# A decoder trunk's first feed-forward: the norm's weights into the transposed input, each token's scale into the results

## The chip, the cores and the metric

The kernel runs on one core of a Trainium2 chip. The metric is the device time of one execution in microseconds, as a median over runs. In the text TensorE does the matrix products, VectorE and ScalarE the elementwise work, GpSimd little beside powers and constants, and SyncE issues the transfers.

## The reference

Two layers run over 256 tokens of width 1024, all in float32. Each layer has a feed-forward, a mixer (a gated recurrence beside windowed attention), a second feed-forward and a gated embedding. Only the start is touched by the change, apart from one move that all four feed-forwards share:

```python
def rmsnorm(x, g):
    xf = x.astype(jnp.float32)
    y = xf * lax.rsqrt(jnp.mean(xf * xf, axis=-1, keepdims=True) + EPS)
    return (y * g.astype(jnp.float32)).astype(x.dtype)

def swiglu(x, w_gate, w_up, w_down):
    return (jax.nn.silu(x @ w_gate) * (x @ w_up)) @ w_down

h = h + 0.5 * swiglu(rmsnorm(h, ffn1_norm), ffn1_w_gate, ffn1_w_up, ffn1_w_down)
```

The scale of a token, the inverse root of its mean square, is one number per row of the input. So it can be applied before the products or to their results; the weight vector `g` has one number per feature, which is a row of the transposed input.

## The kernel before

A product of float32 numbers is made of three faster ones. Every operand is split into a high part (`wh` of the weights, `uT` and so on of the activations; a cast on ScalarE) and a low part (`wl`; a subtraction on VectorE), and TensorE adds high x high, high x low and low x high (`mm3`, line 392; `mm3s`, line 444). So every megabyte of weights is loaded by SyncE into one of two `raw` buffers, split into `wh` and `wl` in pieces of 1024 columns (`feed`, line 332; a ring of 8 pieces), and used by TensorE. A `raw` buffer is loaded anew when VectorE has made the low part of its last piece.

The order of the work on each engine is fixed when the program is written out. A clock of estimated costs (`Clock`, line 61) goes along; background chains (`later`, line 214; `tick`, line 199) are advanced when that clock has passed their ready time, and between two matmuls `feed` splits the next piece of weights if the clock allows.

The program starts in `opening` (line 528). SyncE issues the first 128 rows of x in two halves, the norm's weight vector broadcast over 128 partitions (`gain`, line 523: `g`, 512 KB), the first megabyte of gate weights in four pieces of 256 KB, the other 128 rows of x, and the second megabyte in two pieces. TensorE runs twelve products on a constant tile (`heat`). The mean square of the first rows comes from ScalarE (`sumsq`, line 587) and VectorE, the power from GpSimd (`scale`, line 596), then VectorE makes the normalised rows `xn` (`scaled`, line 603), TensorE transposes them in blocks of 128, and they are split into `uT`. The same is done for the other 128 rows while the first are already multiplied.

The feed-forward (`ffn`, line 653) has three kinds of units. The first 512 features are done with tokens on the partitions: `by_token` (line 663) multiplies a gate unit and an up unit (both named `gu`), applies silu and the product on the results `sg`, and has them transposed by TensorE later (`later_T`, line 519). For the first six pieces `project` (line 398) does the first 128 tokens of a whole unit and then the second. The features behind it come in units of 512 with features on the partitions (`by_feature`, line 694): a gate unit `pg`, silu on ScalarE straight from PSUM (`silu`, line 688), an up unit `pu`, and the product on VectorE (`swiglu`, line 676), which is split into `hid`. There are four full pairs of such units, one of 128 features and a last one of 64. Then the down product `dn` runs over 22 pieces of rows of `w_down` (`down_run`, line 726), at whose start the small loads for the following block are issued.

## Time and profile before

| what | us |
|---|---|
| median of 3 runs (1367.38 to 1368.12) | 1367.64 |
| the profiled execution | 1368.5 |
| its span, first to last instruction | 1366.7 |
| TensorE busy (matmuls) | 1356.1 |
| VectorE busy | 877.4 |
| ScalarE busy | 727.6 |
| first product of the feed-forward starts at | 10.88 |

The page of the profile names engines PE (TensorE's matmuls), PEld (its weight loads), DVE (VectorE), ACT (ScalarE), POOL (GpSimd) and SP (SyncE; SPq is its queue of transfers). L131 is the line of the wrapper that records nearly every instruction, so that rows are told apart by their tiles: `wh<-raw` is the high part of weights made from a loaded buffer. A row of the timeline gives the start, the duration, the engine, the operation, the tiles, the shape and a count, and in brackets the idle time of the engine before it with what ended that. A row of the waits gives who waited for whom, the sum, how often, and the longest. A row of the windows gives for each engine the busy time and the number of instructions, then the clock granted to TensorE as a share of full speed, the busy share of the DMA engines, and what they moved in GB/s.

### The profile page before, as it was taken

To read this page: it belongs to the slowest core of one execution; us is meant where nothing else is said; L and a number is where in the kernel's file an instruction comes from. 1 tells how busy PE (TensorE), PEld (TensorE's weight loads), DVE (VectorE), ACT (ScalarE), POOL (GpSimd) and SP (SyncE) were. 2 spreads that over 40 slices of the span, in tenths; PEclk is the share of its full clock that TensorE was granted. 3 is DMA by queue.
4 is the path that set the end of the run, shared out by engine and by line. 5 is a ranking of instruction groups with operands and counts; after the bars stand their busy time and mean duration, and the time that the engine had idled before them with its cause. 6 is when DMAs were issued, how large, how long until landed. Compare 5 with 4: busy or idle time off the path is not lost.

```text
span 1366.7 us, 21958 instructions
## 1 busy us (share of the span) xinstructions
PE 1356.1 (99%) x9018; PEld 1228.8 (90%) x9018; DVE 877.4 (64%) x1323; ACT 727.6 (53%) x1155; POOL 57.0 (4%) x86
## 2 busy tenths in 40 slices
PE   8999999999999999999999999999999999999998
PEld 6999887899899899988889998878998998899887
DVE  5655458878786665454666554578787876555545
ACT  5454445877565454443565443468785554444433
POOL 1000012000000000000000000120000000000000
PEclk9999999999999999999999999999999999999999
DMA  7765636364645466565466556453556554665651
GB/s 231 228 204 170 233 124 216 97 179 127 222 143 199 146 217 192 168 240 185 154 227 210 181 174 216 140 197 123 155 147 208 164 176 145 210 209 167 243 188 57
DMA packets 126741, 246.44 MB, mean 180 GB/s; under 512 B 15120, under 2 KB 24240, under 8 KB 126640
## 3 DMA queue, kind: packets, MB, share of 16 engines
q1 hardware_dynamic: 126640, 245.03, 56.0%
q8 instruction: 71, 1.16, 0.4%
q14 instruction: 30, 0.25, 0.1%
HBM read 242.91 MB, written 2.10 MB: 179 GB/s over the span
## 4 chain that ended last, share of the span: by engine, by line
PE 96%; DVE 1%; DMA 1%; ACT 1%; issue 0%; POOL 0%; SPq 0%; ACTq 0%; DVEq 0%
PE dn L131 18%; PE pg L131 17%; PE pu L131 14%; PE gt L131 7%; PE z L131 7%; PE gu L131 5%; PE kvq L131 5%; PE ya L131 3%; PE ym L131 3%; PE og L131 3%; PE v L131 3%; PE yo L131 3%; PE tp L131 2%; PE ha L131 1%; PE sc L131 1%; PE pp L131 1%
## 5 line engine op out<-in xcount | busy, mean ns | idle before, releaser
L131 DVE TENSOR_TENSOR wl<-raw,wh 128x1024 fp32r<-128x1024 f32 (+1 forms) x450 | 540.5, 1217 | 345.0 <-ACT wh L131 341.0
L131 ACT CAST wh<-raw 128x1024 fp32r<-128x1024 f32 (+1 forms) x450 | 459.1, 1045 | 407.2 <-PE dn L131 74.6
L131 PE MATMUL dn<-wh,hid 128*128 128x512 f32 x688 | 217.9, 395 | 0.0
L131 PE MATMUL pg<-uT,wh 128*128 128x256 f32 x1088 | 194.3, 281 | 0.0
L131 PE MATMUL pu<-uT,wh 128*128 128x256 f32 x1088 | 193.3, 281 | 0.0
L131 PEld LDWEIGHTS pg<-uT,wh 128*128 128x128 f32 x1088 | 166.7, 188 | 0.3
L131 PEld LDWEIGHTS pu<-uT,wh 128*128 128x128 f32 x1088 | 166.5, 188 | 0.0
L131 PEld LDWEIGHTS dn<-wh,hid 128*128 128x128 f32 x688 | 129.1, 188 | 30.6
L131 PE MATMUL pu<-uT,wl 128*128 128x256 f32 x544 | 152.8, 281 | 0.0
L131 PE MATMUL pg<-uT,wl 128*128 128x256 f32 x544 | 152.8, 281 | 0.0
L131 PE MATMUL dn<-wl,hid 128*128 128x512 f32 x352 | 138.9, 395 | 0.0
L131 PEld LDWEIGHTS pg<-uT,wl 128*128 128x128 f32 x544 | 102.4, 188 | 0.0
L131 PEld LDWEIGHTS pu<-uT,wl 128*128 128x128 f32 x544 | 102.4, 188 | 0.0
L131 PE MATMUL z<-uT,wh 128*128 128x256 f32 x512 | 92.9, 283 | 0.0
L131 PE MATMUL gt<-uT,wh 128*128 128x256 f32 x512 | 92.8, 282 | 0.0
L131 PE MATMUL gu<-wh,uT 128*128 128x512 f32 x256 | 81.2, 401 | 0.0
L131 PEld LDWEIGHTS gt<-uT,wh 128*128 128x128 f32 x512 | 78.8, 188 | 1.3
L131 PEld LDWEIGHTS dn<-wl,hid 128*128 128x128 f32 x352 | 66.1, 188 | 14.9
L131 PEld LDWEIGHTS z<-uT,wh 128*128 128x128 f32 x512 | 78.7, 188 | 0.4
L131 PE MATMUL z<-uT,wl 128*128 128x256 f32 x256 | 71.9, 281 | 0.0
L131 PE MATMUL gt<-uT,wl 128*128 128x256 f32 x256 | 71.8, 281 | 0.0
L131 PE MATMUL kvq<-wh,uT 128*128 128x512 f32 x192 | 63.6, 401 | 0.0
(207 smaller groups left out, 2034.7 us busy)
## 6 DMA issues: line engine op xcount, KB each, us to landing
raw<-in_w_in_dram SPq DMA_DIRECT2D x60, 1024.0 KB
raw<-in_ffn_w_up_dram SPq DMA_DIRECT2D x40, 1024.0 KB
raw<-in_ffn_w_down_dram SPq DMA_DIRECT2D x40, 1024.0 KB
raw<-in_ffn_w_gate_dram SPq DMA_DIRECT2D x38, 1024.0 KB
raw<-in_w_branch_a_dram SPq DMA_DIRECT2D x16, 512.0 KB
raw<-in_w_branch_m_dram SPq DMA_DIRECT2D x8, 1024.0 KB
raw<-in_w_out_dram SPq DMA_DIRECT2D x8, 1024.0 KB
raw<-in_ple_gate_w_dram SPq DMA_DIRECT2D x8, 1024.0 KB
```

The lines of the kernel that those rows point to most:

```text
L131: return issue(*args, **kw)
```

## The change

Only the first feed-forward of the first layer (`opening=True`) takes its input in another form; the other three take part in two smaller edits.

- `opening` no longer broadcasts the weight vector. ScalarE's queue loads it as 8 rows of 128, TensorE transposes that into a column per block of 128 features (`gcol`), and the raw rows of x are transposed. When they are split, ScalarE multiplies each block of 128 x 128 by its column into the high part, and VectorE makes the low part in one operation: four operations of 128 columns on either engine in place of one of 512.
- The mean squares come after that, both halves on ScalarE. The scales of the two groups of tokens are kept (`self.scales`). A small program of TensorE and ScalarE (`spread`) makes from them a tile with the token's scale in every partition.
- With tokens on the partitions the scale goes into the silu's operand and into the product of gate and up. With features on the partitions VectorE multiplies `pg` by the spread tile into SBUF ahead of the silu, and the product of gate and up once more.
- There are five warm-up products in place of twelve and two. A one-column silu stands at the start of ScalarE's order, and the second table load of the opening is gone.
- The second 128 tokens' rows are transposed in two steps within the gate unit (`self.second`, called at the third and at the next to last block of features).
- In all four feed-forwards the product of gate and up of the first units is written as a three-operand operation, and their transposes are entered with a ready time 4 us after the estimated clock (`ready=self.clock.now + 4.0`), so that they stand later in the order.

```diff
--- before.py
+++ after.py
@@ -37,6 +37,7 @@
 AHEAD = (3.0, 2.0)
 ACTIVE = 5
 LAG = 1.5
+WARM = 5
 LATE = 4
 VW = MD + 2
 SLOT = MH * VW
@@ -423,9 +424,12 @@
             for k in range(part.k):
                 kk = k0 + k
                 self.tick()
-                if self.second is not None and kk == KT - 2:
-                    self.finish(self.second)
-                    self.second = None
+                if self.second is not None and kk in (2, KT - 2):
+                    self.advance(self.second)
+                    if self.second in self.bg:
+                        self.second[1] = 1e3
+                    else:
+                        self.second = None
                 xT.wait(kk, t)
                 self.need(part)
                 if kk == 0:
@@ -528,11 +532,13 @@
     def opening(self, vec, xT):
 
 
-        nc, raw, x = self.nc, self.tc.nc, self.a["x"]
+
+        nc, eng, x = self.nc, self.tc.nc, self.a["x"]
+        rows = self.small.tile([P, P], F32, tag="rows", bufs=1, name=self.name("rows"))
+        eng.scalar.dma_start(rows[:KT], vec.rearrange("(k p) -> k p", p=P))
         for n in range(2):
             nc.sync.dma_start(self.h[0][:, half(n)], x[0, :P, half(n)])
         self.clock.load(0.0, 0.5)
-        g = self.gain(vec)
         self.prefetch(1, 4)
         nc.sync.dma_start(self.h[1], x[0, P:, :])
         self.clock.load(0.0, 0.5)
@@ -540,49 +546,57 @@
 
         cold = self.bank("heat")
         heat = self.scr("heat").bitcast(BF16)[:, :NB]
-        raw.vector.memset(heat, 1.0)
-        def warm(n):
-            for _ in range(n):
-                raw.tensor.matmul(cold, heat[:, :P], heat, start=True, stop=True)
-
-        warm(12)
-        ss = [self.col("ss", 2) for _ in range(NT)]
-        self.sumsq(0, 0, ss[0])
-        h = self.h[0][:, half(1)]
-        nc.vector.scalar_tensor_tensor(self.scr("sq"), h, 1.0 / D, h, op0=ALU.mult, op1=ALU.mult,
-                                       accum_out=ss[0][:, 1:2])
-        r = self.scale(ss[0])
-        xn = [self.scaled(0, n, r, g) for n in range(2)]
-        parts = [self.feed(True) for _ in range(2)]
-        tok, ps = slice(0, P), []
+        eng.vector.memset(heat, 1.0)
+        nc.scalar.activation(self.scr("table")[:, :1], heat[:, :1], AF.Silu)
+        for _ in range(WARM):
+            eng.tensor.matmul(cold, heat[:, :P], heat, start=True, stop=True)
+        ps = self.bank("tp")
+        nc.tensor.transpose(ps[:, :KT], rows[:KT], self.ident[:KT, :KT])
+        cols = self.small.tile([P, KT], F32, tag="gcol", bufs=1, name=self.name("gcol"))
+        nc.vector.tensor_copy(cols, ps[:, :KT])
+
+        def put(t, n, ps):
+            for j in range(4):
+                k = n * 4 + j
+                o = (k, slice(t * P, (t + 1) * P))
+                nc.scalar.mul(xT[0](*o), ps[:, j, :], cols[:, k : k + 1])
+                nc.vector.scalar_tensor_tensor(xT[1](*o), ps[:, j, :], cols[:, k : k + 1], xT[0](*o).bitcast(F32),
+                                               op0=ALU.mult, op1=ALU.subtract)
+
+        def scale(t):
+            ss = self.col("ss", 2)
+            for n in range(2):
+                self.sumsq(t, n, ss)
+            return self.scale(ss)
+
+        self.second = self.later(iter(()), 1e3)
+        ps = [self.transposes(self.h[0][:, half(n)], 4) for n in range(2)]
         for n in range(2):
-            ps.append(self.transposes(xn[n], 4))
-            warm(1)
-        put = [self.splitting(xT[0](n * 4, tok, 4), xT[1](n * 4, tok, 4), ps[n]) for n in range(2)]
-        for chain in put:
-            next(chain)
-        parts += [self.feed(True) for _ in range(2)]
-        for n in range(2):
-            self.sumsq(1, n, ss[1])
-        parts += [self.feed(True)]
-        rest = lambda chain: next(chain, None)
-        self.finish(parts[0])
-        rest(put[0])
-        for chain in parts[1:4]:
-            self.finish(chain)
-        rest(put[1])
-        r = self.scale(ss[1])
-        self.finish(parts[4])
-        xn = [self.scaled(1, n, r, g) for n in range(2)]
+            put(0, n, ps[n])
+            for _ in range(2):
+                self.finish(self.feed(True))
+        self.scales = [scale(0)]
         self.finish(self.feed(True))
+        self.bg.remove(self.second)
 
         def second():
             yield
-            for n in range(2):
-                self.to_T(xn[n], xT, n * 4, 1)
-        self.second = self.later(second(), 1e3)
-        xT.written(self.second, 0, KT, 1)
+            put(1, 0, self.transposes(self.h[1][:, half(0)], 4))
+            self.finish(self.feed(True))
+            yield
+            put(1, 1, self.transposes(self.h[1][:, half(1)], 4))
+            self.scales.append(scale(1))
+
+            def spread():
+                ps = self.bank("tp")
+                for t, r in enumerate(self.scales):
+                    nc.tensor.transpose(ps[:, t * P : (t + 1) * P], r.to_broadcast([P, P]), self.ident)
+                yield
+                self.spread = self.small.tile([P, T], F32, tag="spread", bufs=1, name=self.name("spread"))
+                nc.scalar.copy(self.spread, ps[:, :T])
+            self.spreading = self.later(spread(), self.clock.now + 4.0)
+        self.second = self.start(second())
+        self.second[1] = 1e3
 
     def sumsq(self, t, n, ss):
         junk = self.scr("sq")
@@ -666,18 +681,28 @@
             def use(n, t, ps):
                 if n == 0:
                     sg[t] = self.scr("sg")
-                    nc.scalar.activation(sg[t], ps, AF.Silu)
+                    nc.scalar.activation(sg[t], ps, AF.Silu, scale=self.scales[t] if opening else 1.0)
                 else:
-                    nc.vector.tensor_tensor(sg[t], sg[t], ps, op=ALU.mult)
-                    self.later_T(sg[t], hT, 0, t)
+                    nc.vector.scalar_tensor_tensor(sg[t], ps, self.scales[t] if opening else 1.0, sg[t], op0=ALU.mult,
+                                                   op1=ALU.mult)
+                    self.later_T(sg[t], hT, 0, t, ready=self.clock.now + 4.0)
             self.project(units, xT, "gu", use, first=6, group=(2, 4) if opening else (1, 1))
         self.jobs.append(by_token)
 
+        def scaled(out, x):
+
+            k = x.shape[-1] // T
+            out, x = (y.rearrange("p (k t) -> p k t", k=k) for y in (out, x))
+            r = self.spread[: x.shape[0]]
+            nc.vector.tensor_tensor(out, x, r[:, None, :].to_broadcast([x.shape[0], k, T]), op=ALU.mult)
+
         def swiglu(pg, pu, k):
 
 
             for g, u in zip(pg, pu):
                 nc.vector.tensor_tensor(g, g, u, op=ALU.mult)
+                if opening:
+                    scaled(g, g)
             yield
             for i, x in enumerate(pg):
                 n = x.shape[-1] // T
@@ -687,8 +712,12 @@
 
         def silu(ps, p=slice(0, P)):
             out = [self.scr("sg")[p, : x.shape[-1]] for x in ps]
+            if opening:
+                self.finish(self.spreading)
+                for o, x in zip(out, ps):
+                    scaled(o, x[p])
             for o, x in zip(out, ps):
-                nc.scalar.activation(o, x[p], AF.Silu)
+                nc.scalar.activation(o, o if opening else x[p], AF.Silu)
             return out
 
         def by_feature(c0, n):
```

What the edits make of the order is shown at three places. A row is an instruction of one engine, with the tile it writes, the tiles it reads, and the shape; x4 marks four in a row.

ScalarE in the opening, before: `sq` are squares for the norm, `wh` the high parts of gate weights, `uT` those of the transposed input (114 for features 0 to 511, 115 for the others).

```order
L131 ACT_TABLE_LOAD
L131 ACTIVATE sq_254,ss_252<-h_88 128x512
L131 CAST wh_266<-raw_228 128x512
L131 CAST wh_269<-raw_228 128x512
L131 CAST uT_114<-tp_272 128x4x128
L131 CAST uT_115<-tp_278 128x4x128
L131 CAST wh_286<-raw_228 128x512
L131 CAST wh_289<-raw_228 128x512
L131 ACTIVATE sq_292,ss_253<-h_89 128x512
L131 ACTIVATE sq_294,ss_253<-h_89 128x512
L131 CAST wh_296<-raw_234 128x1024
L131 CAST wh_316<-raw_234 128x1024
```

The same place now:

```order
L132 ACTIVATE table_240<-heat_238 128x1
L132 ACTIVATE uT_114<-tp_251,gcol_249 128x128 x4
L132 CAST wh_269<-raw_228 128x512
L132 CAST wh_273<-raw_228 128x512
L132 ACTIVATE uT_115<-tp_256,gcol_249 128x128 x4
L132 CAST wh_285<-raw_228 128x512
L132 CAST wh_289<-raw_228 128x512
L132 ACTIVATE sq_296,ss_295<-h_88 128x512
L132 ACTIVATE sq_298,ss_295<-h_88 128x512
L132 CAST wh_304<-raw_234 128x1024
L132 ACTIVATE uT_114<-tp_315,gcol_249 128x128 x4
L132 CAST wh_328<-raw_234 128x1024
```

Where a cast of 512 to `uT` stood, four copies of 128 stand now, the first four of them ahead of the first cast of weights. The first rows' square has moved behind the fourth cast of weights, where both halves of it stand now; those of the other rows have moved behind the rows shown.

TensorE in the fourth feed-forward, where the gate unit `pg` begins, before: `sg` is the first 128 tokens' result of the first units.

```order
L131 MATMUL pg_12236<-uT_190,wh_12148 128x256
L131 MATMUL pg_12236<-uT_192,wh_12148 128x256
L131 MATMUL pg_12236<-uT_190,wl_12149 128x256
L131 MATMUL pg_12236<-uT_190,wh_12148 128x256
L131 MATMUL pg_12236<-uT_192,wh_12148 128x256
L131 MATMUL pg_12236<-uT_190,wl_12149 128x256
L131 MATMUL tp_12245<-ident,sg_12126 128x128 x4
L131 MATMUL pg_12237<-uT_190,wh_12148 128x256
```

The rows around the same transposes now:

```order
L132 MATMUL pg_12274<-uT_190,wh_12196 128x256
L132 MATMUL pg_12274<-uT_192,wh_12196 128x256
L132 MATMUL pg_12274<-uT_190,wl_12197 128x256
L132 MATMUL pg_12274<-uT_190,wh_12196 128x256
L132 MATMUL pg_12274<-uT_192,wh_12196 128x256
L132 MATMUL pg_12274<-uT_190,wl_12197 128x256
L132 MATMUL tp_12314<-ident,sg_12164 128x128 x4
L132 MATMUL pg_12275<-uT_190,wh_12196 128x256
```

The transposes `tp` of `sg` stood behind the first 6 products of `pg`; now they stand behind 30, in the unit's second piece of weights. A move of this kind is made in the other three feed-forwards too.

VectorE in the first feed-forward, in the first `pg` and `pu` pair, before: `wl` are the low parts of the weights of this and the next unit.

```order
L131 TENSOR_TENSOR wl_557<-raw_476,wh_556 128x1024
L131 TENSOR_TENSOR wl_566<-raw_476,wh_565 128x1024
L131 TENSOR_TENSOR wl_609<-raw_541,wh_608 128x1024
L131 TENSOR_TENSOR wl_624<-raw_541,wh_623 128x1024
L131 TENSOR_TENSOR wl_661<-raw_588,wh_660 128x1024
L131 TENSOR_TENSOR wl_670<-raw_588,wh_669 128x1024
L131 TENSOR_TENSOR sg_617<-sg_617,pu_621 128x512
L131 TENSOR_TENSOR sg_618<-sg_618,pu_622 128x512
L131 TENSOR_TENSOR wl_725<-raw_658,wh_724 128x1024
```

The same place now:

```order
L132 TENSOR_TENSOR wl_593<-raw_506,wh_592 128x1024
L132 TENSOR_TENSOR wl_602<-raw_506,wh_601 128x1024
L132 TENSOR_TENSOR sg_632<-pg_496,spread_427 128x512
L132 TENSOR_TENSOR sg_633<-pg_497,spread_427 128x512
L132 TENSOR_TENSOR wl_653<-raw_577,wh_652 128x1024
L132 TENSOR_TENSOR wl_662<-raw_577,wh_661 128x1024
L132 TENSOR_TENSOR wl_699<-raw_624,wh_698 128x1024
L132 TENSOR_TENSOR wl_708<-raw_624,wh_707 128x1024
L132 TENSOR_TENSOR sg_632<-sg_632,pu_638 128x512
L132 TENSOR_TENSOR sg_632<-sg_632,spread_427 128x512
L132 TENSOR_TENSOR sg_633<-sg_633,pu_639 128x512
L132 TENSOR_TENSOR sg_633<-sg_633,spread_427 128x512
```

The products of `pg` and the spread scale have come in ahead of the next gate unit's low parts, and each product of gate and up is followed by one with the spread scale.

On SyncE the broadcast of the weight vector is gone from the start, and two of the first feed-forward's loads of `w_down` now stand behind the small loads of the mixer's block (`g` of its norm, convolution weights, biases) instead of ahead of them.

## Prediction

> **What bounds the kernel now.** I read the page first, then the waits of TensorE, the chain that ended last, the timeline of the first 40 us, and the one-microsecond windows of the opening.
>
> ```profile
> span 1366.7 us, 21958 instructions
> PE 1356.1 (99%) x9018; PEld 1228.8 (90%) x9018; DVE 877.4 (64%) x1323; ACT 727.6 (53%) x1155; POOL 57.0 (4%) x86
> ```
>
> TensorE is the bound nearly everywhere. A change that leaves its matmuls alone can only win where it waits or runs slowly. All its listed waits:
>
> ```profile
> PE tp L131 <- DVE xn L131: 2.4, 1, 2.4
> PE heat L547 <- DVE heat L543: 1.7, 1, 1.7
> PE tp L131 <- DVE sg L131: 1.6, 1, 1.6
> PE sc L131 <- DVE qT L131: 0.4, 2, 0.2
> PE gu L131 <- DVE wl L131: 0.4, 1, 0.4
> ```
>
> Two places matter: the opening, and one wait for `sg`. The opening on all engines (start, duration; in brackets the idle time before and what ended it):
>
> ```profile
> 0.80 0.86 SPq L533 DMA_DIRECT2D h<-in_x_dram  x2
> ...
> 1.68 5.08 PE L547 MATMUL heat<-heat 128*128 128x512 bf16 x12 [1.68 <-DVE heat L543]
> ...
> 4.59 0.69 DVE L131 SCALAR_TENSOR_TENSOR sq<-h 128x512 f32<-128x512 f32 x1 [2.02 <-DMA h<-in_x_dram]
> ...
> 8.32 1.42 DVE L131 SCALAR_TENSOR_TENSOR xn<-h,r,g 128x512 f32<-128x512 f32 x2 [2.75 <-DMA g<-in_ffn_norm_dram]
> 9.07 1.27 ACT L131 CAST wh<-raw 128x512 fp32r<-128x512 f32 x2 [4.53 <-DMA raw<-in_ffn_w_gate_dram]
> ...
> 10.88 2.15 PE L131 MATMUL gu<-wh,uT 128*128 128x512 f32 x4
> ...
> 11.42 1.14 ACT L131 CAST wh<-raw 128x512 fp32r<-128x512 f32 x2
> ...
> 12.46 0.63 ACT L131 ACTIVATE sq<-h 128x512 f32<-128x512 f32 x1
> ...
> 13.70 1.04 ACT L131 CAST wh<-raw 128x1024 fp32r<-128x1024 f32 x1
> ...
> 14.98 1.05 ACT L131 CAST wh<-raw 128x1024 fp32r<-128x1024 f32 x1 [0.24 <-DMA raw<-in_ffn_w_gate_dram]
> ...
> 15.91 1.41 DVE L131 SCALAR_TENSOR_TENSOR xn<-h,r,g 128x512 f32<-128x512 f32 x2
> ...
> 17.23 1.22 DVE L131 TENSOR_TENSOR wl<-raw,wh 128x1024 fp32r<-128x1024 f32 x1
> ...
> 18.79 0.62 PE L131 MATMUL gu<-wl,uT 128*128 128x512 f32 x2
> ...
> 23.67 2.00 ACT L131 CAST wh<-raw 128x1024 fp32r<-128x1024 f32 x2 [1.06 <-PE gu L131]
> ...
> 24.76 2.36 DVE L131 TENSOR_TENSOR wl<-raw,wh 128x1024 fp32r<-128x1024 f32 x2 [0.89 <-ACT wh L131]
> ```
>
> From the chain that ended last, in order of time:
>
> ```profile
> 1.71 6.46 DMA g<-in_ffn_norm_dram
> ...
> 18.04 18.08 PE gu L131 x78
> ...
> 70.96 11.32 PE pu L131 x96
> ```
>
> The broadcast weight vector `g` was in transfer until 1.71 + 6.46 = 8.17. The normalised rows, their transposes, and the first weights queued behind it all waited. The first product started at 10.88. From 18.04 on TensorE is dense: 18.08 / 78 = 0.232 us for a product of 512 columns. Counting from the two products at 18.79, the gate unit still had 2 + 24 to do (its second tokens' 24 come last), so it ended at 18.79 + 26 x 0.232 = 24.82. Whatever makes that moment earlier, with the weights after it also earlier, shortens the span by as much.
>
> The windows of the opening (TensorE, its weight loads, VectorE, ScalarE, GpSimd; then granted clock, DMA share, GB/s):
>
> ```profile
> 4.00:5.00 1.00, 1.00 (x3) 0.30 (x2) 0.41 (x1) 0.55 (x2) 0.00 (x0) 1.00 1.11 207
> ...
> 9.00:10.00 1.00, 0.88 (x6) 0.70 (x7) 1.00 (x3) 0.90 (x2) 0.00 (x0) 0.91 1.05 420
> ...
> 11.00:12.00 1.00, 1.00 (x4) 0.76 (x4) 1.00 (x2) 1.00 (x3) 0.00 (x0) 0.50 1.04 406
> ...
> 13.00:14.00 1.00, 1.00 (x6) 0.78 (x5) 1.00 (x3) 1.00 (x5) 0.00 (x0) 0.88 0.26 100
> ```
>
> Between 4 and 5 us the DMA engines are as busy as between 11 and 12, but move half as much: `g` is slow by itself. And the first products run at half clock: 0.91 and 0.88 in the outer rows make a low stretch from 9.8 to 13.2, 3.4 us.
>
> **Part A: the opening.** *Transfers.* The second half of x landed by 4.59, the first weight piece by 9.07, the last of the gate unit by 14.98. Between the last two lie nine quarters of a megabyte: 5.91 / 9 = 0.66 us for 256 KB. Without `g` the first piece can land at 4.59 + 0.66 = 5.25 at best; if only the transfer's plain size goes (512 KB, 1.31 us) it lands at 7.76. Because `g` was slow while the engines were busy I take about 5.9, and the rest in step: second rows of x about 9.2, fifth and sixth pieces about 10.5 and 11.8. The 8 x 128 `rows` transfer, of 4 KB, is unseen in this trace; I take it to land no later than x does, 4.59.
>
> *ScalarE and VectorE.* Each half of the transposed x took one 512-wide cast and one subtraction; now it takes four scaled copies and four subtractions of 128. No row has these; the nearest, both on PSUM:
>
> ```profile
> 324.83 0.88 ACT L131 ACTIVATE w<-wt,gcols 128x128 f32<-128x128 f32 x3
> ...
> 337.24 0.62 DVE L131 TENSOR_TENSOR wt<-wt,mask_st 128x128 f32<-128x128 f32 x2
> ```
>
> Back to back that is at most 0.88 / 3 = 0.29 on ScalarE (0.26 from start to start) and 0.31 on VectorE. Four cost about 1.1 and 1.3, where one 512 cast costs 1.14 / 2 = 0.57. So ScalarE pays 0.5 more per half, and VectorE 0.6 (a 512-wide operation is 0.69, in a row of part C); in return VectorE loses the two pairs of `xn` (1.42 and 1.41), the second of which stood ahead of the last gate weights.
>
> In the new order ScalarE does: first scaled copies 5.0 to 6.1 (five warm-ups end at 1.68 + 5 x 0.42 = 3.8; the transposes of the weight vector and of x, and a copy, are an estimate of 1.2 more); two weight casts of 512 to 7.2; four copies to 8.2; two casts to 9.3; the two squares with their read-outs to 10.5 (in the old trace 12.46 to 13.70, 1.24); the fifth piece to 11.5; four copies to 12.5; the sixth piece to 13.5. VectorE follows with the low parts: 11.6 to 12.7, four subtractions to 14.0, and the last gate weights ready at about 15.2, against 17.23 + 1.22 = 18.45.
>
> *TensorE.* First product about 6.7. At the cold rate of 5.08 / 12 = 0.42, the twelve products of k 0 to 3 with four transposes between them last until about 12.8, the clock rises at 13.2 as now, k 4 and 5 last to 14.4, the transposes to 14.9. The last two low products wait for 15.2 or come just after: 15.8. Then 26 x 0.232 = 6.0, and the gate unit ends at 21.8. The new spread transposes add about 0.2 (two of 128 columns). The up unit starts at 22.0 instead of 24.8: **2.8 us**. Its first weights come after four copies and two squares on ScalarE, about 18.5, and 20 with the low part; further ones at 2.00 / 2 = 1.0 and 2.36 / 2 = 1.2 each are ahead of TensorE's 12 x 0.232 = 2.8 per piece. The table load that the order drops ahead of the first `sg` was on ScalarE, off the path. Bounds: without any clock loss the end is 15.2 + 6.0 + 0.2 = 21.4, a gain of 3.4; if small copies cost no more than the casts, some 2 us of ScalarE goes too and it could be 5; if the first piece lands at 7.76 all of it slips 1.7 behind 6.1, and the gain is 1.7.
>
> On the clock the Trainium skill ("TensorE: Matmul & The Clock Gate", section "Why this matters for your kernels") asks for four continuous microseconds of work to get to full clock, and speaks against five warm-ups in place of fourteen. The trace agrees that short work leaves the clock low: 0.50 at 11 us, after twelve warm-ups and an idle gap. By the row alone the sum is the one above, with half clock to 13.2; by the rule alone full clock could come four microseconds after the first product, at 10.7, and part A would be its 3.4 bound.
>
> **Part B: the later transposes of `sg`.** The only long wait behind the opening is in the fourth feed-forward:
>
> ```profile
> 1176.46 0.28 PE L131 MATMUL pg<-uT,wl 128*128 128x256 f32 x1
> 1178.36 0.65 PE L131 MATMUL tp<-ident,sg 128*128 128x128 f32 x4 [1.62 <-DVE sg L131]
> ```
>
> There the first transposes stood after 6 products of `pg`; now they stand after 30. A product of 256 columns takes 11.32 / 96 = 0.118, so 24 of them move the place by 2.8 us, to about 1179.4 on the old clock.
>
> ```profile
> 1177.62 0.68 DVE L131 TENSOR_TENSOR sg<-sg,gu 128x512 f32<-128x512 f32 x1
> ...
> 1179.35 0.68 DVE L131 TENSOR_TENSOR sg<-sg,gu 128x512 f32<-128x512 f32 x1
> ```
>
> `sg` is ready at 1178.30, so the wait of **1.6 us** goes. The second transposes come near 1180.6, after 1180.03: what is late next has half a microsecond. In the other three feed-forwards the place moves without a wait before or behind it: nothing. Multiplying by 1.0 in the other form costs VectorE the same within its rows.
>
> **Part C: the scale on the results.** In each of the first feed-forward's four full gate and up pairs VectorE gets two products ahead of the silu and two behind the up unit.
>
> ```profile
> L131 DVE TENSOR_TENSOR sg<-sg,pu 128x512 f32<-128x512 f32 x32 | 21.7, 686 | 8.0 <-PE pu L131 7.8
> 67.60:90.20 22.60, 22.60 (x194) 22.60 (x193) 14.29 (x14) 12.33 (x14) 0.00 (x0) 1.00 0.68 228
> ```
>
> Four at 0.69 are 2.7 us in a pair of 22.6, in which VectorE worked 14.3. I cost this at nothing: the cover is the up unit of 11.32 us. The new wait is VectorE's for `pg`; behind it stand the next gate unit's four low parts, 2 x 0.69 + 4 x 1.2 = 6.2, wanted 11.3 later. Behind the wait for `pu` stand four products, four low parts and two `hid`, about 9, also in 11.3. On SyncE two `w_down` loads now stand behind the small loads for the mixer:
>
> ```profile
> 136.39 1.20 SPq L525 DMA_DIRECT2D g<-in_mix_norm_dram  x1
> ...
> 144.55 23.30 SPq L328 DMA_DIRECT2D raw<-in_ffn_w_down_dram  x8
> ```
>
> and from the chain:
>
> ```profile
> 136.05 59.81 PE dn L131 x258
> ```
>
> That block lasts 144.55 - 136.39 = 8.2. It now starts two loads earlier, about 133, so the fourth load goes out near 141 and is split by about 148; the down products, from 136.05 at 12 x 59.81 / 258 = 2.8 a part, want it (parts 6 and 7) at 152.8. Cost nothing, with 4 us of cover.
>
> **Sum.** 2.8 + 1.6 = 4.4 us. The profiled execution took 1368.5 us (span 1366.7 and 1.8 around it), so 1364.1; the median shown, 1367.64, is 0.9 lower, which gives **1363.2 us**.
>
> **The rivals.** *1. The clock stays low.* TensorE's work between 6.7 and 15 us has gaps, and a clock raised one window later costs half of it: the low stretch in the old trace is 3.4 us long, so 1.7 us each. One more window leaves a gain of 2.7: **1364.9**; two leave 1.0: **1366.6**. For it: half clock after twelve warm-ups now. Against it: the old trace recovered at 13.2 with gaps of the same sort, and cold products fill the time. The Trainium skill ("TensorE: Matmul & The Clock Gate", section "What's actually happening") has the clock judged in windows of about 3.4 us, and the low stretch agrees with that. Chance 0.14.
>
> *2. The weights do not come earlier by more than the size of `g`.* Part A gives 1.7, with B 3.3: **1364.3**. Against it stands 207 GB/s at a DMA share of 1.11 between 4 and 5 us. Chance 0.15.
>
> *3. Slower: VectorE in the first feed-forward.* If the conversions behind the waits for `pg` and `pu` do not fit in one unit, TensorE waits for `wl` at each pair. It decides where the work behind a wait, 6.2 and 9 us, passes 11.3, as it would if the raw loads, issued only when VectorE frees their buffers, land late in the unit. At 2 us for each of four pairs it costs 8, less 4.4 gained: **1371.2**. For it: VectorE gets a fifth more work and a place in front of its weights. Against it: 22.60 of 22.60 busy on TensorE now, and 8 us of idle VectorE. Chance 0.06.
>
> *4. B does not go, or moves into a new wait of the same size.* Gain 2.8: **1364.8**. The margin is 1.1 us by rows. Chance 0.07.
>
> **How the numbers follow.** The forecast keeps 0.58. The range takes in A from 1.7 to some 4.2 with B, and the first clock case: **1361.8 to 1366.4**. About 0.2% (2.7 us) is what a measurement of this kernel can tell from no change: faster by that is under 1364.9. The forecast, four fifths of case 2 and a third of 1 and of 4 lie there: 0.77. No change: the rest of 1, 2 and 4, and a little of 3: 0.18. Slower: the rest of 3, 0.05.
>
> **What would show it.** Right: no `g` transfer; the first `wh` cast near 6 instead of 9.07; first product near 6.7; the last gate `wl` ready near 15; the up unit from about 22; no wait for `sg` near 1175; no TensorE wait for `wl` before 200 us. Wrong: the granted clock at 0.50 beyond 14 us; TensorE waiting for `wl` or for `wh` after 25 us; a first cast later than 7.8.

## The result, and the profile after

The changed kernel takes **1371.73 us** (median of 7 runs, 1371.60 to 1373.36); the kernel before takes 1367.64 (7 runs beside them, 1367.13 to 1369.22). The ratio is 1.0031, with a 95% interval of 1.0020 to 1.0043: slower by about 4.1 us, where 4.4 us of gain were forecast. The profiled execution took 1372.26 us, with a span of 1370.0; that of before took 1368.5, with 1366.7. From the page of after:

```profile
span 1370.0 us, 22000 instructions
...
PE 1357.4 (99%) x9012; PEld 1230.2 (90%) x9012; DVE 888.3 (65%) x1350; ACT 731.3 (53%) x1170; POOL 59.2 (4%) x86
```

TensorE is still the bound. Its waits in after:

```profile
PE gu L132 <- ACT wh L132: 6.0, 4, 2.9
PE heat L552 <- DVE heat L549: 1.7, 1, 1.7
...
```

The waits for `xn` (2.4) and for `sg` (1.6) are gone, as forecast. In their place stands the first row: four waits, 6.0 us together, for gate weights that ScalarE converts. All four lie in the opening. The opening of after on the three engines (start, duration; in brackets the idle time before and what ended it):

```profile
5.28 0.37 ACT L132 ACTIVATE uT<-tp,gcol 128x128 fp32r<-128x128 f32 x1 [2.38 <-PE tp L132]
5.68 0.35 DVE L132 SCALAR_TENSOR_TENSOR uT<-tp,gcol,uT 128x128 fp32r<-128x128 f32 x1 [1.28 <-ACT uT L132]
6.07 0.37 ACT L132 ACTIVATE uT<-tp,gcol 128x128 fp32r<-128x128 f32 x1 [0.42 <-DVE uT L132]
6.47 0.35 DVE L132 SCALAR_TENSOR_TENSOR uT<-tp,gcol,uT 128x128 fp32r<-128x128 f32 x1 [0.43 <-ACT uT L132]
6.86 0.37 ACT L132 ACTIVATE uT<-tp,gcol 128x128 fp32r<-128x128 f32 x1 [0.42 <-DVE uT L132]
...
7.64 0.37 ACT L132 ACTIVATE uT<-tp,gcol 128x128 fp32r<-128x128 f32 x1 [0.42 <-DVE uT L132]
7.91 1.13 ACT L132 CAST wh<-raw 128x512 fp32r<-128x512 f32 x2
...
8.57 2.17 PE L132 MATMUL gu<-wh,uT 128*128 128x512 f32 x4 [2.87 <-ACT wh L132]
...
19.73 1.22 DVE L132 TENSOR_TENSOR wl<-raw,wh 128x1024 fp32r<-128x1024 f32 x1 [0.58 <-ACT wh L132]
...
27.14 0.38 PE L132 MATMUL tp<-ident,r 128*128 128x128 f32 x2
```

Read the brackets of the small operations: each copy on ScalarE but the first waits 0.42 us for VectorE's subtraction of the block before (`<-DVE uT`), and each subtraction 0.43 us for ScalarE's copy. The two engines take turns. A copy starts every 0.79 us (5.28, 6.07, 6.86, 7.64), though it lasts 0.37; the cast behind the last one starts at 7.91, in a place where 6.1 was forecast. This happens four times. The gate unit's last low part is ready at 19.73 + 1.22 = 20.95 (forecast 15.2; before 18.45), and the up unit starts behind the two transposes of 27.14.

The granted clock of after in the opening (TensorE, its weight loads, VectorE, ScalarE, GpSimd; then granted clock, DMA share, GB/s):

```profile
8.00:9.00 1.00, 0.43 (x1) 0.29 (x1) 0.80 (x2) 1.00 (x4) 0.00 (x0) 0.78 1.02 375
...
11.00:12.00 1.00, 1.00 (x5) 0.80 (x4) 0.35 (x1) 0.58 (x3) 0.00 (x0) 0.51 0.06 23
```

It is one low stretch of 3.4 us, as before: 0.78 and 0.51 in the outer rows put it from 8.56 to 11.98. Where the time came from, by the start of the first feed-forward's `pg` products (count, shortest/median/longest ns, first and last start), before and after:

```profile
L131 PE MATMUL pg<-uT,wh x18: 274/282/365, 36.0 to 39.8; 128*128 128x256 f32 x18
```

```profile
L132 PE MATMUL pg<-uT,wh x20: 277/280/284, 38.5 to 41.9; 128*128 128x256 f32 x20
```

The opening costs 38.5 - 36.0 = 2.5 us, where it was to gain 2.8. The rest arises far behind it. The second layer's mixer and the gate and up products of the fourth feed-forward behind it, each from its first product to the next stage's first (columns as in the clock's table), before:

```profile
877.92:1152.73 274.81, 274.61 (x1911) 251.01 (x1910) 213.80 (x421) 177.31 (x343) 17.93 (x25) 1.00 0.53 165
1152.73:1274.69 121.96, 120.34 (x929) 115.82 (x928) 67.54 (x70) 57.80 (x70) 1.47 (x1) 1.00 0.58 184
```

and after:

```profile
880.64:1156.97 276.33, 276.14 (x1911) 251.94 (x1910) 213.96 (x421) 177.13 (x343) 19.09 (x25) 1.00 0.53 164
1156.97:1278.21 121.24, 121.24 (x929) 116.69 (x928) 67.66 (x70) 58.33 (x70) 1.46 (x1) 1.00 0.58 183
```

The mixer is 1.52 us longer with the same products, the same clock and the same waits. In the fourth feed-forward the 1.62 us of waiting are gone (busy 120.34 of 121.96 before, all of 121.24 after), but the busy time rose by 0.90. From the chain that ended last, a unit of 96 products there, before and after:

```profile
1257.90 11.31 PE pu L131 x96
```

```profile
1261.25 11.41 PE pu L132 x96
```

The products follow each other 0.9% more slowly. No step of the prediction has that.

### The profile page after: what moved, and what is told of

It is laid out like the page before. It is cut to its first block, busy times and chain, and to the rows that moved or that the text cites. A ratio compares the mean times of both kernels' runs of the same rounds, so it can differ in the third digit from the quotient of the medians.

```text
span 1370.0 us, 22000 instructions
## 1 busy us (share of the span) xinstructions
PE 1357.4 (99%) x9012; PEld 1230.2 (90%) x9012; DVE 888.3 (65%) x1350; ACT 731.3 (53%) x1170; POOL 59.2 (4%) x86
## 4 chain that ended last, share of the span: by engine, by line
PE 98%; DVE 1%; ACT 1%; issue 0%; ACTq 0%
PE dn L132 18%; PE pg L132 17%; PE pu L132 14%; PE gu L132 7%; PE gt L132 7%; PE z L132 7%; PE kvq L132 5%; PE ya L132 3%; PE ym L132 3%; PE yo L132 3%; PE og L132 3%; PE v L132 3%; PE tp L132 2%; PE ha L132 1%; PE sc L132 1%; PE pp L132 1%
## 5 line engine op out<-in xcount | busy, mean ns | idle before, releaser
L132 PEld LDWEIGHTS gu<-wh,uT 128*128 128x128 f32 x256 | 48.0, 190 | 18.8 <-ACT wh L132 7.7
```

The source lines that it names most:

```text
L132: return issue(*args, **kw)
```

## The experiments

Eleven kernels ran, each beside runs of the kernel before on its chip. The kernel before had medians of 1367.48 (e1 to e4), 1367.43 (e5 to e8) and 1367.42 (e9 to e11). Theory P, on which the first runs rest: the copies and subtractions alternate because of the order in which they are written, and that alone turns part A from a gain into a loss.

**e1_copies_first.** Of the changed kernel's `put`, the four copies are written ahead of the four subtractions; nothing else.

```
-            for j in range(4):
-                k = n * 4 + j
-                o = (k, slice(t * P, (t + 1) * P))
-                nc.scalar.mul(xT[0](*o), ps[:, j, :], cols[:, k : k + 1])
+            at = [(n * 4 + j, slice(t * P, (t + 1) * P)) for j in range(4)]
+            for j, o in enumerate(at):
+                nc.scalar.mul(xT[0](*o), ps[:, j, :], cols[:, o[0] : o[0] + 1])
+            for j, o in enumerate(at):
                 nc.vector.scalar_tensor_tensor(
...
```

> The changed kernel with one edit: in each group ScalarE's four copies into the high part are written out ahead of VectorE's four subtractions, so that no copy waits for a subtraction. Theory P (in the changed kernel each copy but the first waits for VectorE's subtraction of the block before, 0.79 us from copy to copy in place of about 0.27): copies come 0.26 to 0.30 apart, the last low part of the gate weights is ready at about 15.5 in place of 20.95, the up unit starts at about 22 in place of 27.3, and the time falls by about 5 us, from 1371.7 to about 1366.5. Rival Q (it is the number of small operations, the five warm-ups or the new place of the transposes, and the waits only fill time that would be idle anyway): the up unit stays within 1 us of 27 and the time stays at 1371. Rival R (some 2 us of the loss lie in the second layer, where TensorE's products stand about 1% further apart in the changed kernel's trace): whatever the opening does, the stretch from 946 to 1270 us stays longer by 2 us than in the kernel before.

Measured: 1366.25 us (11 runs, 1365.91 to 1367.54), ratio to before 0.9991 (0.9982 to 1.0000). That is 5.5 us under the changed kernel, with the same instructions. Its opening:

```profile
5.28 1.14 ACT L132 ACTIVATE uT<-tp,gcol 128x128 fp32r<-128x128 f32 x4 [2.38 <-PE tp L132]
...
6.46 1.12 DVE L132 SCALAR_TENSOR_TENSOR uT<-tp,gcol,uT 128x128 fp32r<-128x128 f32 x4 [2.05 <-ACT uT L132]
...
6.98 2.25 PE L132 MATMUL gu<-wh,uT 128*128 128x512 f32 x4 [0.88 <-ACT wh L132]
...
12.00 1.20 PE L132 MATMUL gu<-wh,uT 128*128 128x512 f32 x4
...
14.16 1.21 DVE L132 TENSOR_TENSOR wl<-raw,wh 128x1024 fp32r<-128x1024 f32 x1
...
21.55 0.38 PE L132 MATMUL tp<-ident,r 128*128 128x128 f32 x2
```

Four copies take 1.14 us and four subtractions 1.12: the forecast's 1.1 and 1.3. The first product comes at 6.98 (forecast 6.7), the last low part is ready at 15.37 (15.2), and the up unit starts behind the transposes at about 21.7 (22.0). The forecast's sum fits this kernel, not the one that was changed. The windows show a granted clock of 1.00 in every microsecond here, but that is not full speed from the start: the first four products take 2.25 us, four of the same kind at 12.00 take 1.20. The trace has no record of the clock before 10.4 us, and a window without a record is shown as 1.00. Theory P holds. But the time is only 1.2 us under before, so something else still costs.

**e2_before_late_sg.** Part B alone: the kernel before with the later place of the transposes.

```
-                    self.later_T(sg[t], hT, 0, t)
+                    self.later_T(sg[t], hT, 0, t, ready=self.clock.now + 4.0)
```

> The kernel before with one part of the change: the ready time 4 us after the estimated clock for the transposes of the first units' result. Part B of the prediction: the wait of 1.6 us in the fourth feed-forward goes and the time is 1366.0, 1.6 less. Rival: the wait comes back at another instruction, and the time stays at 1367.6. Rival R: the second layer's spacing of products is a property of one execution and not of the order, so that it may differ here too.

Measured: 1367.11 us (11 runs, 1366.83 to 1368.49), ratio 1.0000 (0.9991 to 1.0009). No gain that can be measured, though the wait for `sg` is not in its profile.

**e3_after_early_sg.** The reverse: the changed kernel without `ready=self.clock.now + 4.0`.

> The changed kernel without that ready time. Part B: the wait for sg near 1180 us is back, and the time is about 1.7 higher than the changed kernel's, 1373.4. Rival: no difference, 1371.7.

Measured: 1373.05 us (5 runs, 1371.47 to 1373.50), ratio 1.0036 (1.0024 to 1.0049). Its profile (the run of 1371.47) has no wait for `sg`, and its fourth feed-forward is as long as in after. The medians lie 1.3 us apart, close to the 1.7 that was expected, but four of the five runs lie between 1372.8 and 1373.5, where two of the seven of after lie too, and none of these was profiled. So it stays open here; e9 asks again on another kernel.

**e4_no_scale_on_features.** The changed kernel without the spread scale; it leaves out the scaling of the later units of the first feed-forward (`scaled` in `swiglu` and `silu`, and `spread`).

> The changed kernel without the token's scale on the results that have features on the partitions (it leaves out the spread tile, the multiplication of the gate results ahead of the silu and that of the products; the first 512 features keep theirs). Part C of the prediction (VectorE's added work is covered by the up unit): the time stays within 0.3 us of the changed kernel's, 1371.7. Rival C (the longer way from PSUM through VectorE to ScalarE costs TensorE time that the list of waits does not show): faster by 1 us or more.

Measured: 1372.05 us (9 runs, 1369.87 to 1372.46), ratio 1.0028 (1.0018 to 1.0038). That is the changed kernel's time, as forecast, but the median alone does not settle it: most runs lie near 1370.0 or near 1372.2, and this kernel also differs in a second thing (below). The traces do: the later units of the first feed-forward, 96 products each, last 11.34 us with the scale (after) and without it (e4). In after TensorE is busy without a gap in the stretch that the prediction looked at:

```profile
67.60:90.20 22.60, 22.60 (x193) 22.60 (x193) 14.35 (x17) 10.26 (x13) 0.00 (x0) 1.00 0.55 186
```

One thing was odd. The second mixer, which the edit does not touch, took 275.58 us here, 276.33 in after, 276.32 in e1, 276.34 in e3, but 274.81 in before and 274.78 in e2. Since after, e1 and e3 agree to 0.02 us, it is no accident of one execution. The built programs (not the trace) show what these kernels have in common: the large tiles lie in 22 slots of SBUF (`self.slots`), and which slot a tile gets follows from the order in which tiles are first written and set free. In after, e1 and e3 eight slots are exchanged against before, in e4 two, in e2 none. That the slot sets the pace of the products is theory S.

**e5_slots_back.** e1, and three tiles are claimed early by memsets (fills with a constant) of one column on GpSimd (the first and the second tile of the opening's high parts, the first of the next block's). The instructions of the other engines keep their order; only two slots are still exchanged.

```
+        self.tc.nc.gpsimd.memset(xT[0](0)[:, :1].bitcast(F32), 0.0)
+        self.tc.nc.gpsimd.memset(xT[0](4)[:, :1].bitcast(F32), 0.0)
...
+                    self.tc.nc.gpsimd.memset(following[1][0](0)[:, :1].bitcast(F32), 0.0)
```

> This is the kernel with the four copies first (1366.25 us), and three one-column memsets on GpSimd that claim three tiles early; the order on all other engines stays instruction for instruction. What changes is which of the 22 slots in SBUF a tile gets: in the changed kernel eight of the slots are exchanged against the kernel before, here only two are. In the changed kernel and in the one with copies first the second layer's mixer takes 276.33 us against 274.81 before, and its last gate and up stage has units of 11.41 us against 11.31. Theory S (the slots that the tiles get set how fast the products run): the mixer goes back to 274.8 +- 0.3 and the units to 11.31, and the time to 1366.25 - 1.5 - 0.7 = 1364.0 us (1363.5 to 1364.7). Rival I (the slower products belong to the program itself: more operations on the other engines, the other form of the multiplication): mixer 276.3, units 11.41, 1366.2 us.

Measured: **1363.96 us** (7 runs, 1363.58 to 1364.60), ratio 0.9973 (0.9962 to 0.9984): the best kernel of the study with e9, 3.5 us under before. The two stages in e5:

```profile
874.76:1149.46 274.70, 274.49 (x1912) 250.91 (x1911) 213.88 (x421) 177.14 (x343) 17.86 (x25) 1.00 0.53 165
1149.46:1270.13 120.67, 120.67 (x930) 116.36 (x928) 67.54 (x70) 58.01 (x70) 1.46 (x1) 1.00 0.58 184
```

The mixer is back at before's length. In the built programs of e1 and e5 every tile outside the slots has the same place. Of the fourth feed-forward 0.57 us come back, not all: its units take 11.37, and its transposed x has one of the two slots that are still exchanged.

**e6_before_slots_moved.** The kernel before, with nine slots exchanged (not ten, as the expectation has it) by six memsets on GpSimd: two claims, and four dummy tiles that are written once. The order on TensorE, VectorE, ScalarE and SyncE is the same.

```
+                    for _ in range(4):
+                        self.tc.nc.gpsimd.memset(self.slot("dummy")[:, :1], 0.0)
```

> This is the kernel before, with six tiny memsets on GpSimd (two claim tiles of the opening, four write dummy tiles once); the order on TensorE, VectorE, ScalarE and SyncE stays instruction for instruction. Ten of the 22 slots are exchanged by it; the last tile of the fourth feed-forward's transposed x comes to lie in the slot in which the changed kernel has it (the second of the 22, in place of the seventh). Theory S (slots): the second layer's mixer and the units of the fourth feed-forward change by some tenths of a per cent, most likely to slower: units 11.35 to 11.41, mixer 275 to 276.4; time 1368 to 1370 us. Rival I (program): mixer 274.8, units 11.31, time as before, 1367.5 +- 0.5.

Measured: 1367.70 us (11 runs, 1366.52 to 1368.71), ratio 1.0003 (0.9993 to 1.0012). By the total nothing happened. By stages, a good deal:

```profile
880.10:1155.45 275.35, 275.14 (x1911) 251.38 (x1910) 213.92 (x421) 176.86 (x343) 18.05 (x25) 1.00 0.52 165
1155.45:1275.20 119.75, 119.75 (x930) 115.31 (x929) 67.75 (x70) 57.91 (x70) 1.46 (x1) 1.00 0.58 187
```

From the chain of e6, two units of the fourth feed-forward:

```profile
1247.25 11.22 PE pg L131 x96
1258.47 11.27 PE pu L131 x96
```

The mixer is 0.54 longer than in before, the units of the fourth feed-forward are shorter (11.22 and 11.27 against 11.31). I had expected that stage to become slower. That slots change the pace of the products is borne out; which slot is good is not known.

**e7_after_more_warm.** The changed kernel with ten more warm-up products behind the first eight transposes of x.

```
+        for _ in range(10):
+            eng.tensor.matmul(cold, heat[:, :P], heat, start=True, stop=True)
```

> This is the changed kernel with ten more warm-up products behind the first eight transposes of x, so that TensorE has no gap of 2.5 us before its first product. Theory P (the alternation of small copies and subtractions sets the opening; the low clock between 8.6 and 12.0 us is hidden behind it): the granted clock stays at 1.00, the first product still starts at 8.6, the gate unit's last low part is ready at 20.9 as before, the up unit starts at 27.2 and the time is the changed kernel's, 1371.7 us within 0.5. Rival C (the half clock costs its 1.7 us): 1370.0 us.

Measured: 1371.79 us (6 runs, 1371.67 to 1372.95), ratio 1.0032 (1.0020 to 1.0044): the changed kernel's time. Its low stretch did not go, against what I expected, but moved behind the next gap, to 13.3 to 16.7:

```profile
13.00:14.00 1.00, 0.97 (x3) 0.72 (x3) 0.91 (x2) 1.00 (x4) 0.00 (x0) 0.66 0.00 0
...
16.00:17.00 1.00, 1.00 (x5) 0.78 (x4) 0.80 (x2) 0.17 (x1) 0.00 (x0) 0.64 0.99 373
```

and the up unit starts where it did (27.14 in after):

```profile
27.17 0.38 PE L132 MATMUL tp<-ident,r 128*128 128x128 f32 x2
```

The small operations set the pace: in after, from the start of the first copy to the end of the gate unit's last low part (5.28 to 20.95 us), neither ScalarE nor VectorE waits for TensorE.

**e8_weights_first.** e5 with the first piece of weights converted ahead of the first four copies.

```
+        self.finish(self.feed(True))
         for n in range(2):
             put(0, n, ps[n])
-            for _ in range(2):
+            for _ in range(n + 1):
                 self.finish(self.feed(True))
```

> This is the kernel of e5_slots_back with the first piece of gate weights converted ahead of the first four scaled copies, on ScalarE and on VectorE. In the kernel with the copies first ScalarE stands idle until 5.28 us, while the first weight piece has landed, by the moved bytes, near 5.0; VectorE is busy without a gap from 7 to 11 us and 12 to 15 us, and TensorE waits for it three times by some 0.4 us. Theory P: the chain of VectorE starts 0.6 earlier, first product near 6.3 in place of 6.98, and the time is that of e5_slots_back less 0.4 (0 to 0.7). Rival (the first piece lands only near 5.8, as the transfers were thought to do): the copies start later by 0.5, first product 7.3, and the time is 0.3 over that of e5_slots_back.

Measured: 1364.57 us (9 runs, 1363.60 to 1364.98), ratio 0.9977 (0.9968 to 0.9987): no better than e5, though the first product starts at 6.4 and in the profiles the `pg` products start 0.3 earlier (32.8, in e5 33.1); theory P's gain of 0.4 is not found. But it shows when the first piece lands, since here ScalarE waits for it:

```profile
5.46 0.62 ACT L132 CAST wh<-raw 128x512 fp32r<-128x512 f32 x1 [2.55 <-DMA raw<-in_ffn_w_gate_dram]
```

At 5.46, against the 5.9 of the forecast and its bounds of 5.25 and 7.76.

**e9_slots_back_early_sg.** e5 with part B undone.

> This is the kernel of e5_slots_back (1363.96 us) with part B undone: the transposes of the first gate and up units stand where they stood before. Theory B (the later place saves TensorE a wait of some 1.6 us in the fourth feed-forward, in the executions in which the up unit's weights are converted late): 1364.0 + 0.4 to 1.6, so 1364.9 (1364.4 to 1365.6), and a wait for sg in the profile where the conversion of the up weights begins less than a microsecond ahead of the first pg product. Rival N (in the changed opening the weights come early enough anyway, as in the profile of e3_after_early_sg, where no wait for sg was left): 1364.0 +- 0.4, no wait for sg.

Measured: 1363.85 us (8 runs, 1363.50 to 1366.31), ratio 0.9976 (0.9966 to 0.9987). Part B is worth nothing that can be measured here. Its fourth feed-forward, in which the transposes again stand behind six products:

```profile
1169.70 2.00 ACT L132 CAST wh<-raw 128x1024 fp32r<-128x1024 f32 x2 [0.75 <-DMA raw<-in_ffn_w_up_dram]
...
1172.19 0.40 PE L132 MATMUL pg<-uT,wh 128*128 128x256 f32 x2
...
1172.90 0.60 PE L132 MATMUL tp<-ident,sg 128*128 128x128 f32 x4
```

There is no wait. The same place in the profile of before, which has one:

```profile
1175.39 2.00 ACT L131 CAST wh<-raw 128x1024 fp32r<-128x1024 f32 x2 [2.34 <-DMA raw<-in_ffn_w_up_dram]
...
1175.87 0.40 PE L131 MATMUL pg<-uT,wh 128*128 128x256 f32 x2
```

and in e6, which has before's order:

```profile
1175.94 2.00 ACT L131 CAST wh<-raw 128x1024 fp32r<-128x1024 f32 x2 [2.64 <-DMA raw<-in_ffn_w_up_dram]
...
1178.69 0.40 PE L131 MATMUL pg<-uT,wh 128*128 128x256 f32 x2
```

In each the cast of the up weights ends an idle time that a transfer ended. In e9 it begins 2.49 us ahead of the first `pg` product, in e6 2.75 ahead; in the twelve profiles other than before's it is 2.06 to 2.80. In the profile of before it is 0.48. VectorE takes the weights' low part first, so its product `sg` came some 2 us late, once. Of the four profiles with before's place of the transposes (before, e3, e6, e9), one has the wait that part B removes. How often executions without a profile have it is not shown.

**e10_after_slots_back.** The changed kernel with the three claims of e5.

> This is the changed kernel as it is, with the alternating copies, and the three claims of e5_slots_back. Theory S (the slots that the tiles get are worth 1.5 us in the second mixer and 0.6 in the last gate and up stage): 1371.73 - 2.2 = 1369.5 us (1369.0 to 1370.2); mixer of the second layer 274.7, units of the fourth feed-forward 11.37. Rival: the gain of e5 came only together with the shorter opening; 1371.7 us.

Measured: 1370.88 us (11 runs, 1369.32 to 1371.69), ratio 1.0024 (1.0015 to 1.0033): 0.85 under the changed kernel, where 2.2 were expected. The stages did what theory S says:

```profile
881.88:1156.61 274.73, 274.52 (x1912) 250.92 (x1910) 213.79 (x421) 177.09 (x343) 17.91 (x25) 1.00 0.53 165
1156.61:1277.29 120.68, 120.68 (x929) 116.35 (x928) 67.60 (x70) 58.28 (x70) 1.46 (x1) 1.00 0.58 184
```

That is 1.60 and 0.56 less than in after. In this execution the first stage lost 1.1 of them: the low stretch of the clock fell where TensorE was dense.

```profile
20.00:21.00 1.00, 1.00 (x4) 0.48 (x3) 1.00 (x2) 0.02 (x1) 0.00 (x0) 0.76 0.00 0
...
23.00:24.00 1.00, 1.00 (x4) 0.81 (x3) 0.35 (x1) 1.00 (x4) 0.00 (x0) 0.53 0.97 358
```

It lasts from 20.5 to 23.9; the first stage is 128.23 us long here and 127.26 in after, and begins 0.14 later.
That the other runs lost the missing 1.4 us in the same way is not shown.

**e11_copies_one_ahead.** The changed kernel with each copy written one place ahead of the subtractions: copy 0, copy 1, subtraction 0, copy 2, subtraction 1, copy 3, subtractions 2 and 3.

> This is the changed kernel with each scaled copy written one place ahead: copy 0, copy 1, subtraction 0, copy 2, subtraction 1, copy 3, subtractions 2 and 3. Theory W (an operation waits for whatever was written ahead of it on the other engine with the same tile, whichever block it touched): copies 2 and 3 still wait for a subtraction; from the first copy's start to the last one's end about 2.2 us in place of 2.7 in the changed kernel and 1.14 with all copies first; per group of four 0.5 us less than in the changed kernel, and the time lies a third of the way to the kernel with copies first: 1371.73 - 1.5 to 2.0, about 1370 us (1369.3 to 1370.8). Rival K (a copy waits only for its own block): copies without a gap, 1.14 us, and 1366.3 us. Rival Q (the two engines can't read the same bank of PSUM at a time, whatever the order): 2.7 us a group and 1371.7 us.

Measured: 1369.92 us (11 runs, 1369.51 to 1371.25), ratio 1.0017 (1.0008 to 1.0026), and

```profile
5.28 0.62 ACT L132 ACTIVATE uT<-tp,gcol 128x128 fp32r<-128x128 f32 x2 [2.37 <-PE tp L132]
5.94 0.35 DVE L132 SCALAR_TENSOR_TENSOR uT<-tp,gcol,uT 128x128 fp32r<-128x128 f32 x1 [1.54 <-ACT uT L132]
6.32 0.37 ACT L132 ACTIVATE uT<-tp,gcol 128x128 fp32r<-128x128 f32 x1 [0.42 <-DVE uT L132]
6.73 0.35 DVE L132 SCALAR_TENSOR_TENSOR uT<-tp,gcol,uT 128x128 fp32r<-128x128 f32 x1 [0.44 <-ACT uT L132]
7.11 0.37 ACT L132 ACTIVATE uT<-tp,gcol 128x128 fp32r<-128x128 f32 x1 [0.42 <-DVE uT L132]
```

From 5.28 to 7.48 are 2.2 us, as theory W says. Copy 1, written straight behind copy 0, does not wait. The first subtraction, which needs block 0 alone, waits for both copies (5.90 is the end of the second). And copies 2 and 3 wait for the subtraction written ahead of them. So the wait follows the tile and the order of writing, not the block, and not the bank of PSUM, which all of them read. The built programs say the same of the first group: in after each copy but the first carries a wait for the count that the subtraction ahead of it raises, in e1 no copy behind the first has a wait and the first subtraction waits for the count of the fourth copy, and in e11 for that of the second. The turns are written into the program; they are no property of the two engines.

## Why the prediction was wrong, point by point

- **Part A, the cost of the small operations: this is the step that failed.** The prediction put it so: "Four cost about 1.1 and 1.3". The sizes were about right (1.14 and 1.12 in e1), and the places reckoned from them fit the order of e1 within 0.3 us. What failed is "first scaled copies 5.0 to 6.1": the four were taken as back to back, while `put` writes copy, subtraction, copy, subtraction, all with one tile for the high parts. The order of ScalarE that the prediction was worked from has the four copies in a row; it is VectorE's subtractions between them, on the other engine, that each copy waits for. From the first copy's start to the operation behind the fourth it took 2.63 us (5.28 to 7.91) in place of about 1.1, and in the last group 3.49 (19.60 to 23.09). It is 5.5 us of the total (e1). One of the prediction's signs of being wrong showed it, a first cast later than 7.8 (7.91), but that sign was meant for late weights.
- **Part A, the rest.** Without that wait the opening gains what was forecast. In e5, whose `pg` products are these, it is 36.0 - 33.1 = 2.9 us against 2.8. That the two agree so closely is in part luck: with before's opening these products start at 36.0, 36.8 (e2) or 36.7 (e6), with the copies first at 32.9 (e1), 33.1 or 32.7 (e9), so the gain is 2.9 to 4.1.

```profile
L132 PE MATMUL pg<-uT,wh x17: 276/280/281, 33.1 to 35.9; 128*128 128x256 f32 x17
```

- **The transfers.** Right in kind: without `g` the first piece lands at 5.46, sooner than the 5.9 that was taken. Rival 2 is out. Its sum was off besides: a slip of 1.7 leaves 1.1 of the 2.8, and the 1.7 that stands there only of the 3.4 without clock loss.
- **The clock.** One low stretch, as the forecast assumed, though at 8.6 to 12.0 and not to 13.2. It was not on the path in after (e7), so rival 1 is not what made it slower. With the copies first no low stretch follows a full one (e1, e5, e8, e9); in e1 the first products run at half speed until 10.4, and its opening is as early as that of e5, which is at full speed from 6.2. The prediction read the 0.50 at 11 us as short work leaving the clock low. The records of before have full speed from 6.4 to 9.8, behind twelve warm-ups of 5.08 us, and the low stretch only behind the wait of 2.4 us. The Trainium skill ("TensorE: Matmul & The Clock Gate", section "What's actually happening") has the clock judged in free-running windows of about 3.4 us. The traces agree with the length (3.41 us, and twice that in e2) and with its place changing (8.6 in after, 20.5 in e10, whose order on TensorE is the same; 13.3 in e7).
- **Part B.** The later place does take the wait away, but the price was wrong: the 1.6 us stood in one profile, where a transfer came late. e2 and e9 show no gain, the profile of e6 has before's order and no wait, and e3 stays open (1.3 us, within the spread). The profiled execution was 0.9 us over the median; the prediction noted that and still took all of the wait off the median.
- **Part C and the loads.** Nothing, as forecast (e4, and no wait in the down product of after); rival 3 is out. That its 1371.2 lies near the measured time is chance.
- **What no step had.** The prediction put the stages that the edits do not touch at nothing. The slots changed them: 2.3 us from e1 to e5 in the medians, 2.2 by the two stages of e10, of which its median shows 0.85. From the changed kernel 5.5 us go with the order of the copies (e1) and 2.3 more with the slots (e5); what is left of the change then gains 3.5 us on the kernel before (ratio 0.9973), most of it part A (2.9 in the profiles).

## What to carry to other kernels

Before costing a row of small operations as back to back, read for each what it waits for in the written order: two engines whose operations on one tile are written by turns wait for each other in that order, whichever block each touches, at the price of both plus two hand-overs, unless one engine's operations are all written first. A wait of one profiled execution that ends on a transfer is worth its share of the executions, which one profile does not tell. And when an edit moves the time of stages that it does not touch, compare stage by stage with two other edits of the same kernel before calling it noise.

## What the runs showed of the hardware that was not expected

- **The pace of products depends on where tiles lie.** With the same instructions in the same order on TensorE, VectorE, ScalarE and SyncE, 96 products of 256 columns in the fourth feed-forward took 11.31 us (before) or 11.22 and 11.27 (e6), and the second mixer 276.32 (e1) or 274.70 (e5). The Trainium skill ("SBUF — State Buffer", section "Who interferes with whom") says that TensorE never waits on another engine for SBUF. No run here shows such a wait or rules it out. The runs do not show what makes the difference, only that the place does: a rule for good slots stays open. Slots are also not all of it: e2 has before's slots, and its fourth feed-forward, 120.53 us without a wait, was busy 0.19 us longer than the 120.34 of before.
- **A hand-over between ScalarE and VectorE** costs little by itself: 0.37 + 0.35 us of work make 0.79 us from copy to copy, so some 0.03 each. What is lost is the overlap: four copies in a row start some 0.26 us apart ((1.14 - 0.37) / 3).
- **A low stretch of the clock is worth what TensorE has to do in it:** nothing in after and e7, where it waits for weights anyway, and 1.1 us in e10.
- **Half a window of work kept the clock up.** Cut into stretches of 3.41 us from where the clock records begin, the openings of the thirteen profiles show full speed lost behind stretches in which TensorE was busy, by the profile, for 0.16 (after), 0.31 (before), 0.41 (e10) or 0.50 (e7, 9.9 to 13.3) of the time, and kept behind 0.50 (e7, 16.7 to 20.1), 0.62 (e5) or more. So a wait of 2.00 us cost e10 the clock, while the same wait in after, which fell across two such stretches (0.67 and 0.70), did not.
